# First modulation of a diffusion block: split products against plain fp32 products in four column groups

## Chip, core and metric

One NeuronCore of a Trainium2 chip runs the whole program. The metric is device time in microseconds (us) of one execution. The kernel before takes 2560.0 us, the median of 3 runs (2559.35 to 2563.09).

## What is computed

One layer of a diffusion backbone in fp32: 512 latent tokens (an 8 x 64 grid) and 256 context tokens of width 2048. A linear map of SiLU(c), or of SiLU(c_ctx) for the context, gives six vectors of 2048; the first two, shift and scale, modulate the input before the attention. That map, for these two vectors, is what the change touches.

```python
def ada_params(cond, w, b):
    return jnp.split(jax.nn.silu(cond) @ w + b, N_ADA, axis=-1)
def modulate(x, shift, scale):
    return x * (1 + scale) + shift
sh1, sc1, g1, sh2, sc2, g2 = ada_params(c, ada_w, ada_b)
csh1, csc1, ... = ada_params(c_ctx, ada_w, ada_b)
h, hc = modulate(x, sh1, sc1), modulate(ctx, csh1, csc1)
q, k, v = split(h @ w_qkv);  k_c, v_c = split(hc @ w_qkv[:, D_MODEL:])
x = layer_norm(alpha * x + g1 * (attention(q, k, v, k_c, v_c) @ w_o))
x = layer_norm(alpha * x + g2 * swiglu(modulate(x, sh2, sc2)))
```

## The kernel before

Everything is kept transposed, channels on partitions, in tiles of 128 channels; `kt` counts the 16 of them. Large products run as three matmuls on fp32r operands: each fp32 operand is split by `split` (lines 76 to 78) into a rounded part `hi` (a cast on ScalarE) and the rest `lo` (a subtraction on VectorE), and `mm3` adds hi*hi, hi*lo and lo*hi in PSUM. Weights arrive by `unit` (lines 103 to 106): a load of 128 x 1024 on SyncE's queue into one of six buffers of the pool `p0`, then the split into `wh_...` and `wl_...`, of which there are three each.

The first stage (lines 236 to 245) goes over `kt`. For each it needs shift and scale of 128 channels, for latent and context.

- `ada_start(kt)` (lines 182 to 193) computes them as rows. The stationary operand is `sil`, for each of the 16 tiles of the contraction four columns: SiLU(c) and SiLU(c_ctx), each as hi and lo part. The moving operand is 256 columns of the weights (128 shifts, 128 scales), once as hi and once as lo. That makes 4 units of weights and 32 matmuls into four rows of PSUM bank 7 (`adp`), copied by ScalarE to `row`.
- `ada_cols(kt)` (lines 195 to 205) turns the rows to columns by two transposes on TensorE, and two additions on VectorE join the hi and lo parts and the bias in `md`.
- `h_start(kt)` (lines 207 to 218) modulates 128 channels of x and of the context on VectorE and splits them (`a_h`, `hc`).
- `qkv_start(kt)` (lines 220 to 234) multiplies them with a 128 x 768 weight tile (`w0`; `wh_w`, `wl_w`) into seven banks `acc`: 12 matmuls of 512 columns, then 18 of 256.

The modulation of kt+1 stands ahead of the main products of kt, and `ada_cols(kt + 1)` between the 512-column and the 256-column ones:

```python
for kt in range(KT):
    h_start(kt)
    if kt + 1 < KT:
        ada_start(kt + 1)
    qkv_start(kt)
```

The framework's scheduler sets the final order of each engine's queue from this order and the buffers; it moves single instructions past each other, among them loads of the next stage's value weights (`wr_v`), which it puts among those of this stage.

Of the kernel before, what the change touches and what calls it, by code (L numbers as in the profile page):

```python
# [9 lines left out]
F32 = mybir.dt.float32  # L10
F32R = mybir.dt.float32r
AF = mybir.ActivationFunctionType
ALU = mybir.AluOpType
# [4 lines left out]
P = 128  # L18
D = 2048
KT = D // P  # L20
# [13 lines left out]
U = 1024  # L34
# [9 lines left out]
def build(tc, ins, out):  # L44
    nc = tc.nc
    with ExitStack() as top:
        base = top.enter_context(tc.tile_pool(name="base", bufs=1))
# [4 lines left out]
        def bank(i, name):  # L52
            return psp.tile([P, T], F32, tag=f"b{i}", name=name)
# [7 lines left out]
        def any_bank(name):  # L61
            turn["all"] += 1
            return bank((turn["all"] - 1) % 8, name)
# [12 lines left out]
        def split(hi, lo, src):  # L76
            nc.scalar.copy(hi, src)  # L77
            nc.vector.tensor_tensor(out=lo, in0=src, in1=hi.bitcast(F32), op=ALU.subtract)  # L78

        def mm(ps, a, b, start, stop):  # L80
            nc.tensor.matmul(ps, a, b, start=start, stop=stop, skip_group_check=True)  # L81
# [9 lines left out]
        def raw_tile(name, tag=None):  # L91
            if tag is None:
                tag = rtags[0][rtags[1] % len(rtags[0])]
                rtags[1] += 1
            return rp[0].tile([P, U], F32, tag=tag, name=f"wr_{name}", bufs=RAWBUFS.get(tag))

        def pieces(raw, name, n=U):
            hi = wp.tile([P, U], F32R, tag="whi", name=f"wh_{name}")
            lo = wp.tile([P, U], F32R, tag="wlo", name=f"wl_{name}")
            split(hi[:, :n], lo[:, :n], raw[:, :n])  # L100
            return hi, lo

        def unit(src, name, n=U):
            raw = raw_tile(name)
            nc.sync.dma_start(raw[:, :n], src)
            return pieces(raw, name, n)

        cv = base.tile([P, 2, KT], F32, name="cv")
        nc.sync.dma_start(cv, ins["cv"])
        nc.scalar.activation(cv, cv, AF.Silu)  # L110
        sil = base.tile([P, KT, 4], F32R, name="sil")
        for i in range(2):
            split(sil[:, :, 2 * i], sil[:, :, 2 * i + 1], cv[:, i])
        ada = base.tile([P, 64], F32, name="ada")
        ident = base.tile([P, P], F32, name="ident")
        make_identity(nc, ident)
        ones = base.tile([P, P], F32, name="ones")
        nc.gpsimd.memset(ones, 1.0 / D)
        eps_t = base.tile([P, 1], F32, name="eps_t")
# [3 lines left out]
        bin1 = base.tile([P, KT, 4], F32, name="bin1")  # L123
        bin2 = base.tile([P, 64], F32, name="bin2")

        def biases():
            nc.vector.tensor_copy(bin1, pv[:, 128:192].rearrange("p (k f) -> p k f", f=4))
            nc.vector.tensor_scalar_add(bin1[:, :, 2:4], bin1[:, :, 2:4], 1.0)
            nc.vector.tensor_copy(bin2, pv[:, 0:64])
            nc.vector.tensor_scalar_add(bin2[:, 32:48], bin2[:, 32:48], 1.0)  # L130
# [22 lines left out]
        with ExitStack() as ph1:  # L153
            pa = ph1.enter_context(tc.tile_pool(name="pa", bufs=1))
# [27 lines left out]
            def ada_start(kt):  # L182
                ps = bank(7, f"adp{kt}")
                for u in range(4):
                    hi, lo = unit(ins["ada_n"][kt, :, u * U:(u + 1) * U], f"an{kt}_{u}")
                    for jj in range(4):
                        j = u * 4 + jj
                        s_ = slice(jj * 256, jj * 256 + 256)
                        mm(ps[:4, :256], sil[:, j], hi[:, s_], j == 0, False)
                        mm(ps[:4, :256], sil[:, j], lo[:, s_], False, j == KT - 1)  # L190
                row = pa.tile([4, 256], F32, tag="row", name=f"row{kt}")
                nc.scalar.copy(row, ps[:4, :256])
                rows[kt] = (ps, row)

            def ada_cols(kt):
                ps, row = rows.pop(kt)
                pc = ps[:, 256:264].rearrange("p (f c h) -> p f c h", f=2, c=2)
                for i in range(2):
                    nc.tensor.transpose(ps[:, 256 + 4 * i:260 + 4 * i], row[:, i * P:(i + 1) * P], ident[:4, :4])
                md = pa.tile([P, 4], F32, tag="md", name=f"md{kt}", bufs=2)  # L200
                mdv = md.rearrange("p (f c) -> p f c", f=2)
                nc.vector.tensor_tensor(out=mdv, in0=pc[:, :, :, 0], in1=bin1[:, kt].rearrange("p (f c) -> p f c", f=2),
                                        op=ALU.add)
                nc.vector.tensor_tensor(out=mdv, in0=pc[:, :, :, 1], in1=mdv, op=ALU.add)
                mods[kt] = md

            def h_start(kt):
                md = mods.pop(kt)
                xr = stage(f"xr{kt}")
                nc.gpsimd.dma_start(xr, ins["xT"][kt])  # L210
                nc.vector.tensor_scalar(out=xr, in0=xr, scalar1=md[:, 2:3], scalar2=md[:, 0:1],
                                        op0=ALU.mult, op1=ALU.add)
                split(*new_act(kt, "h"), xr)
                cr = stage(f"cr{kt}")
                nc.gpsimd.dma_start(cr[:, :C], ins["ctxT"][kt])
                nc.vector.tensor_scalar(out=cr[:, :C], in0=cr[:, :C], scalar1=md[:, 3:4], scalar2=md[:, 1:2],
                                        op0=ALU.mult, op1=ALU.add)
                split(hc_hi[kt], hc_lo[kt], cr[:, :C])
# [16 lines left out]

            with tc.tile_pool(name="p0", bufs=6) as p0:
                rp[0] = p0
                ada_start(0)
                biases()
                ada_cols(0)  # L240
# [5 lines that stand above are left out]
# [173 lines left out]
            for hp in range(1, NH // 2):  # L419
# [6 lines left out]
                for i in range(2):  # L426
                    h = hp * 2 + i
# [42 lines left out]
        with ExitStack() as ph2:  # L470
# [96 lines left out]
            for n in range(KT - 1):  # L567
                if n < 3:
                    ps = ys[n]
                else:  # L570
                    ps = any_bank(f"y{n}")
# [5 lines left out]
            for cs in (HA, HB):  # L577
                ps = any_bank(f"y{KT - 1}_{cs.start}")[:, HA]
                for kt in range(KT):
                    hi, lo = hl[kt // 8]  # L580
                    s_ = slice(kt % 8 * P, kt % 8 * P + P)
# [327 lines left out]
            for cs in (HA, HB):  # L909
                for n in range(KT):  # L910
                    u = cu[n // 2][:, n % 2 * T:n % 2 * T + T]
# [68 lines left out]
```

## Time and profile before

| | |
|---|---|
| median of 3 runs | 2560.0 us (2559.35 to 2563.09) |
| profiled execution, its own time | 2558.94 us |
| its span in the trace | 2557.2 us |
| TensorE granted clock, mean | 0.987 |
| DMA | 395.66 MB, mean 155 GB/s |
| first stage (first product to last of `acc`) | 8.3 to 165.5 us |

The span is what the trace covers of the profiled execution. Engines: PE is TensorE's matmuls and PEld its weight loads, which overlap them; DVE is VectorE, ACT ScalarE, POOL GpSimd, SP SyncE. `L81` is line 81; since one helper records all matmuls, tile names tell them apart. A record's duration is its latency, and matmuls are pipelined: how fast they follow each other is read from their starts. `128*4` ahead of a shape is the stationary operand, partitions x columns.

### The profile page before, as it was taken

The numbers are of one execution on the slowest core, as the hardware profiler recorded it, in microseconds if no ns is written. First come the engines' busy times: TensorE is split into PE (matmuls) and PEld (weight loads), VectorE is DVE, ScalarE is ACT, GpSimd is POOL, SyncE is SP. The second block draws the span as 40 slices with busy tenths as digits, with TensorE's granted clock in tenths as the row PEclk, the third lists the DMA queues.
The fourth block names the chain that finished last, engine by engine and source line by source line (L and its number), as shares of the span: only waits on it lengthen the run. The fifth ranks groups of instructions, "written<-read, shape, count | busy, mean of one in ns | idle before, by whom it ended". The sixth has DMA issues, their size and how long they took to land.

```text
span 2557.2 us, 44451 instructions
## 1 busy us (share of the span) xinstructions
PE 2455.8 (96%) x18124; PEld 2305.1 (90%) x18124; DVE 1880.4 (74%) x2742; ACT 1074.9 (42%) x1640; POOL 220.6 (9%) x334
## 2 busy tenths in 40 slices
PE   8999999999999999999999999999999989999994
PEld 5788989898898987889999999999999989999984
DVE  7886665565565565459887887888878877878888
ACT  5662322222232244227544444444444534546444
POOL 1110000000010000001110110101101000000002
PEclk9999999999999999999999999999999999999997
DMA  9965454444444464214443334333444654755542
GB/s 332 308 211 168 148 165 133 156 160 151 154 157 156 144 234 145 92 64 141 148 141 117 134 127 138 131 122 130 138 138 160 201 173 126 214 146 159 133 121 75
DMA packets 137294, 395.66 MB, mean 155 GB/s; under 512 B 16416, under 2 KB 40368, under 8 KB 136960
## 3 DMA queue, kind: packets, MB, share of 16 engines
q1 hardware_dynamic: 116992, 342.42, 40.2%
q0 software_dynamic: 20096, 50.39, 7.2%
q8 instruction: 142, 2.33, 0.4%
q14 instruction: 64, 0.52, 0.1%
HBM read 351.85 MB, written 40.89 MB: 154 GB/s over the span
## 4 chain that ended last, share of the span: by engine, by line
PE 55%; issue 26%; DVE 9%; DMA 7%; ACT 2%; POOL 2%; SPq 0%; POOLq 0%; ACTq 0%; DVEq 0%
PE y L81 6%; DMA wr_ada<-ada_t 6%; PE qp L81 5%; PE kp L81 5%; PE vp L81 4%; PE acc L81 3%; PE cp L81 2%; DVE wr_ada L138 2%; PE o L81 1%; PE adp L81 1%; DVE wl_v L78 1%; PE f31b L81 1%; PE f28b L81 1%; PE f24b L81 1%; PE f21b L81 1%
## 5 line engine op out<-in xcount | busy, mean ns | idle before, releaser
L721 DVE TENSOR_TENSOR wr_f<-wr_f,wr_f 128x1024 f32<-128x1024 f32 x164 | 199.9, 1219 | 1.4
L81 PE MATMUL vp<-wh_v,a_h 128*128 128x256 f32 x896 | 167.9, 279 | 0.0
L81 PE MATMUL y<-a_o,wh_o 128*128 128x512 f32 (+1 forms) x544 | 163.0, 383 | 0.0
L138 DVE CUSTOM_DVE_ANT_0 wr_ada<-wr_ada,s_c,bin 128x1024 f32<-128x1024 f32 x64 | 83.5, 1304 | 86.8 <-DMA wr_ada<-ada_t 86.5
L81 PEld LDWEIGHTS vp<-wh_v,a_h 128*128 128x128 f32 x896 | 141.3, 188 | 0.6
L81 PE MATMUL kp<-a_h,wh_k 128*128 128x512 f32 x448 | 141.1, 396 | 0.0
L81 PE MATMUL qp<-a_h,wh_q 128*128 128x512 f32 x448 | 140.6, 395 | 0.0
L138 DVE CUSTOM_DVE_ANT_0 wr_ada<-wr_ada,s_c,adap 128x1024 f32<-128x1024 f32 x64 | 82.2, 1284 | 74.6 <-DMA wr_ada<-ada_t 74.5
L81 PE MATMUL vp<-wl_v,a_h 128*128 128x256 f32 x448 | 125.1, 279 | 0.0
L81 PEld LDWEIGHTS y<-a_o,wh_o 128*128 128x128 f32 x544 | 99.7, 188 | 21.7 <-ACT wh_o L77 0.7
L721 DVE TENSOR_TENSOR wr_g<-wr_g,wr_g 128x896 f32<-128x896 f32 (+1 forms) x96 | 107.6, 1131 | 6.1 <-DMA wr_g<-w_out 5.1
L77 ACT CAST th<-tr 128x256 fp32r<-128x256 f32 (+2 forms) x96 | 45.9, 478 | 151.4 <-PE tr L316 148.3
L81 PE MATMUL y<-a_o,wl_o 128*128 128x512 f32 (+1 forms) x272 | 104.0, 382 | 0.5 <-DVE wl_o L78 0.5
L81 PEld LDWEIGHTS cp<-hc,wh_k 128*128 128x128 f32 x448 | 84.1, 188 | 20.2
L81 PE MATMUL vp<-wh_v,hc 128*128 128x256 f32 x512 | 99.4, 283 | 0.0
L81 PEld LDWEIGHTS qp<-a_h,wh_q 128*128 128x128 f32 x448 | 82.1, 188 | 16.4
L634 POOL DMA_DIRECT2D setB<-h x66 | 35.6, 542 | 700.8 <-DVE h L773 689.0
L78 DVE TENSOR_TENSOR tl<-tr,th 128x256 fp32r<-128x256 f32 (+2 forms) x96 | 52.9, 552 | 54.3 <-ACT th L77 54.2
L81 PE MATMUL cp<-hc,wh_k 128*128 128x256 f32 x448 | 89.5, 281 | 0.0
L78 DVE TENSOR_TENSOR wl_an<-wr_an,wh_an 128x1024 fp32r<-128x1024 f32 x64 | 76.2, 1224 | 18.2 <-ACT wh_an L77 17.8
L81 PE MATMUL qp<-a_h,wl_q 128*128 128x512 f32 x224 | 88.6, 396 | 0.0
L299 ACT ACTIVATE p<-sc,sm 128x256 f32<-128x256 f32 x64 | 30.3, 474 | 138.4 <-DVE sm L297 138.3
(1666 smaller groups left out, 8461.0 us busy)
## 6 DMA issues: line engine op xcount, KB each, us to landing
wr_f<-w_in SPq DMA_DIRECT2D x164, 512.0 KB, 4.2
wr_ada<-ada_t SPq DMA_DIRECT2D x128, 512.0 KB, 4.0
wr_an<-ada_n SPq DMA_DIRECT2D x64, 512.0 KB, 6.2
wr_g<-w_out SPq DMA_DIRECT2D x64, 448.0 KB, 4.5
wr_v<-w_v SPq DMA_DIRECT2D x32, 512.0 KB, 4.7
wr_o<-w_o SPq DMA_DIRECT2D x32, 512.0 KB, 3.8
wr_g<-w_out SPq DMA_DIRECT2D x32, 512.0 KB, 4.3
wr_q<-w_qk SPq DMA_DIRECT2D x28, 512.0 KB, 4.5
```

The lines of the kernel that those rows point to most:

```text
L77: nc.scalar.copy(hi, src)
L78: nc.vector.tensor_tensor(out=lo, in0=src, in1=hi.bitcast(F32), op=ALU.subtract)
L81: nc.tensor.matmul(ps, a, b, start=start, stop=stop, skip_group_check=True)
L138: nc.vector.tensor_tensor_reduce(out=raw, in0=raw, in1=s_c[:, half * U:(half + 1) * U], scale=1.0, scalar=bin2[:, i:i + 1] if half == 0 el ...
L299: nc.scalar.activation(p[:, nl:nl + C], sc[:, :C], AF.Exp, bias=sm[:, 2:3], accum_out=sm[:, 3:4])
L634: nc.gpsimd.dma_start(setD[n][q], src)
L721: nc.vector.tensor_tensor(out=self.r[out][:, :n], in0=self.r[a][:, :n], in1=self.r[b][:, :n], op=op)
```

## The change

The weights of the first modulation are no longer split. The products are plain fp32. The 16 tiles of the contraction go in turn to four groups of 32 columns of the array: tile j = 4u + g is multiplied in group g and added up, over the units u, in the 32 rows of PSUM that begin at 32g. The stationary operand `sil` has 32 columns for each tile, the first two SiLU(c) and SiLU(c_ctx), the others zero, so that all 128 rows are written. `row` has 128 rows. In place of the two transposes stand two fp32 products with `sel`, a 128 x 2 matrix of zeros and ones that adds rows 0, 32, 64 and 96 into column 0 and rows 1, 33, 65 and 97 into column 1. One addition with the bias is left.

```diff
-        sil = base.tile([P, KT, 4], F32R, name="sil")
-        for i in range(2):
-            split(sil[:, :, 2 * i], sil[:, :, 2 * i + 1], cv[:, i])
...
+        sel = base.tile([P, 2], F32, name="sel")
+        nc.vector.tensor_tensor(out=sel, in0=ident[:, 0:2], in1=ident[:, 32:34], op=ALU.add)
+        for g in (64, 96):
+            nc.vector.tensor_tensor(out=sel, in0=sel, in1=ident[:, g:g + 2], op=ALU.add)
...
             def ada_start(kt):
                 ps = bank(7, f"adp{kt}")
                 for u in range(4):
-                    hi, lo = unit(ins["ada_n"][kt, :, u * U:(u + 1) * U], f"an{kt}_{u}")
-                    for jj in range(4):
-                        j = u * 4 + jj
-                        s_ = slice(jj * 256, jj * 256 + 256)
-                        mm(ps[:4, :256], sil[:, j], hi[:, s_], j == 0, False)
-                        mm(ps[:4, :256], sil[:, j], lo[:, s_], False, j == KT - 1)
-                row = pa.tile([4, 256], F32, tag="row", name=f"row{kt}")
-                nc.scalar.copy(row, ps[:4, :256])
+                    raw = raw_tile(f"an{kt}_{u}")
+                    nc.sync.dma_start(raw, ins["ada_n"][kt, :, u * U:(u + 1) * U])
+                    for g in range(4):
+                        mm(ps[32 * g:32 * g + 32, :256], sil[:, u * 4 + g], raw[:, g * 256:g * 256 + 256],
+                           u == 0, u == 3)
+                row = pa.tile([P, 256], F32, tag="row", name=f"row{kt}")
+                nc.scalar.copy(row, ps[:, :256])
                 rows[kt] = (ps, row)
...
                 for i in range(2):
-                    nc.tensor.transpose(ps[:, 256 + 4 * i:260 + 4 * i], row[:, i * P:(i + 1) * P], ident[:4, :4])
+                    mm(ps[:, 256 + 2 * i:258 + 2 * i], row[:, i * P:(i + 1) * P], sel, True, True)
                 md = pa.tile([P, 4], F32, tag="md", name=f"md{kt}", bufs=2)
-                mdv = md.rearrange("p (f c) -> p f c", f=2)
-                nc.vector.tensor_tensor(out=mdv, in0=pc[:, :, :, 0], in1=bin1[:, kt].rearrange("p (f c) -> p f c", f=2),
-                                        op=ALU.add)
-                nc.vector.tensor_tensor(out=mdv, in0=pc[:, :, :, 1], in1=mdv, op=ALU.add)
+                nc.vector.tensor_tensor(out=md, in0=ps[:, 256:260], in1=bin1[:, kt], op=ALU.add)
...
             with tc.tile_pool(name="p0", bufs=6) as p0:
                 rp[0] = p0
+                sil = p0.tile([P, KT, 32], F32, name="sil", bufs=1)
+                nc.gpsimd.memset(sil, 0.0)
+                for i in range(2):
+                    nc.vector.tensor_copy(sil[:, :, i], cv[:, i])
```

TensorE's queue before, where the main products of the first kt end and the modulation of the third begins (a row gives line, output and operands, the shape of the output, and how often it repeats):

```order
L81 MATMUL acc_126<-hc_89,wl_w_271 128x256
L81 MATMUL adp_319<-wh_an_0_322,sil 4x256
L81 MATMUL adp_319<-wl_an_0_323,sil 4x256
L81 MATMUL adp_319<-wh_an_0_322,sil 4x256
L81 MATMUL adp_319<-wl_an_0_323,sil 4x256
```

The same place with the change, up to the main products of the second kt and the selecting products among them:

```order
L81 MATMUL acc_125<-hc_88,wl_w_209 128x256
L81 MATMUL adp_256<-wr_an_0_257,sil 32x256 x4
L81 MATMUL adp_256<-wr_an_1_263,sil 32x256 x4
L81 MATMUL adp_256<-wr_an_2_269,sil 32x256 x4
L81 MATMUL adp_256<-wr_an_3_275,sil 32x256 x4
L81 MATMUL acc_119<-a_h,wh_w_285 128x512 x2
...
L81 MATMUL acc_122<-a_h,wl_w_286 128x512
L81 MATMUL adp_256<-sel,row_281 128x2 x2
L81 MATMUL acc_123<-wh_w_285,a_h 128x256
```

Eight products of two operands for each unit became four, one for each column group, which read the landed weights themselves.

VectorE's queue before, from the modulation of the second kt to that of the third (`an2` and `an3` are weight units, `w01` the main weights):

```order
L202 TENSOR_TENSOR md1_288<-adp1_209,bin1_86 128x4
L204 TENSOR_TENSOR md1_288<-adp1_209,md1_288 128x4
L211 TENSOR_SCALAR xr1_309<-xr1_309,md1_288 128x512
L216 TENSOR_SCALAR cr1_314<-cr1_314,md1_288 128x256
L78 TENSOR_TENSOR a0_h_201<-xr1_309,a0_h_201 128x512
L78 TENSOR_TENSOR hc0_89<-cr1_314,hc0_89 128x256
L78 TENSOR_TENSOR wl_an2_2_351<-wr_an2_2_348,wh_an2_2_350 128x1024
L78 TENSOR_TENSOR wl_an2_3_365<-wr_an2_3_362,wh_an2_3_364 128x1024
L78 TENSOR_TENSOR wl_w01_381<-wr_w01_378,wh_w01_380 128x768
L78 TENSOR_TENSOR wl_an3_0_433<-wr_an3_0_430,wh_an3_0_432 128x1024
L78 TENSOR_TENSOR wl_an3_1_447<-wr_an3_1_444,wh_an3_1_446 128x1024
```

And now, the whole round:

```order
L200 TENSOR_TENSOR md2_303<-adp2_256,bin1_85 128x4
L207 TENSOR_SCALAR xr2_323<-xr2_323,md2_303 128x512
L212 TENSOR_SCALAR cr2_328<-cr2_328,md2_303 128x256
L78 TENSOR_TENSOR a0_h_171<-xr2_323,a0_h_171 128x512
L78 TENSOR_TENSOR hc1_89<-cr2_328,hc1_89 128x256
L78 TENSOR_TENSOR wl_w02_363<-wr_w02_360,wh_w02_362 128x768
```

The four subtractions of 1024 columns and the second addition are gone from it. In SyncE's queue the three first loads of `wr_v`, which stood among the weight units of the modulation, now stand behind the last `wr_w` of the stage.

## Rows read from the trace of the kernel before

**Rows 1.** The page of the kernel before: busy us of each engine, share of the span, instructions.

```profile
PE 2455.8 (96%) x18124; PEld 2305.1 (90%) x18124; DVE 1880.4 (74%) x2742; ACT 1074.9 (42%) x1640; POOL 220.6 (9%) x334
```

**Rows 2.** Busy time per stretch; after each colon: length, engines, clock, DMA share, GB/s.

```profile
4.00:20.00 16.00, 9.81 (x52) 5.57 (x53) 10.62 (x18) 9.57 (x14) 0.00 (x0) 0.89 1.02 401
21.93:156.67 134.74, 129.50 (x902) 99.78 (x901) 110.86 (x156) 84.99 (x115) 15.51 (x30) 1.00 0.88 302
```

**Rows 3.** Instructions on tile adp: duration ns min/median/max, first and last start.

```profile
L81 PEld LDWEIGHTS adp<-wh_an,sil x256: 82/84/125, 8.3 to 155.3; 128*4 128x4 f32 x128
...
L192 ACT COPY row<-adp x16: 352/354/363, 14.6 to 156.7; 4x256 f32<-4x256 f32 x16
```

**Rows 4.** Timeline of TensorE, one kt; start us, duration us, idle before it.

```profile
42.90 0.63 PE L81 MATMUL acc<-a_h,wh_w 128*128 128x512 f32 x2
43.36 0.40 PE L81 MATMUL acc<-a_h,wl_w 128*128 128x512 f32 x1
43.69 0.28 PE L199 MATMUL adp<-ident,row 4*128 4x4 f32 x2
43.90 0.39 PE L81 MATMUL acc<-wh_w,a_h 128*128 128x256 f32 x1
...
46.01 0.28 PE L81 MATMUL acc<-hc,wl_w 128*128 128x256 f32 x1
46.13 0.28 PE L81 MATMUL adp<-wh_an,sil 128*4 128x256 f32 x1
...
47.96 0.28 PE L81 MATMUL adp<-wh_an,sil 128*4 128x256 f32 x1
48.62 0.28 PE L81 MATMUL adp<-wl_an,sil 128*4 128x256 f32 x1 [0.38 <-DVE wl_an L78]
...
49.43 0.28 PE L81 MATMUL adp<-wh_an,sil 128*4 128x256 f32 x1
49.54 0.40 PE L81 MATMUL acc<-a_h,wh_w 128*128 128x512 f32 x1
```

**Rows 5.** TensorE's waits, 22 to 160 us: us in total, times, longest.

```profile
PE adp L81 <- DVE wl_an L78: 5.2, 14, 0.4
```

**Rows 6.** Timeline of all engines, the start and the first kt.

```profile
5.78 1.04 ACT L77 CAST wh_an<-wr_an 128x1024 fp32r<-128x1024 f32 x1 [3.17 <-DMA wr_an<-ada_n]
...
8.33 0.37 PE L81 MATMUL adp<-wh_an,sil 128*4 128x256 f32 x1 [8.33 <-DVE sil L78]
...
11.07 1.05 ACT L77 CAST wh_an<-wr_an 128x1024 fp32r<-128x1024 f32 x1 [0.44 <-DMA wr_an<-ada_n]
...
14.59 0.35 ACT L192 COPY row<-adp 4x256 f32<-4x256 f32 x1
...
21.93 0.36 ACT L192 COPY row<-adp 4x256 f32<-4x256 f32 x1
```

**Rows 7.** Loads of tile wr_an and what is made from it.

```profile
L77 ACT CAST wh_an<-wr_an x64: 1039/1048/1053, 5.8 to 152.2; 128x1024 fp32r<-128x1024 f32 x64
L78 DVE TENSOR_TENSOR wl_an<-wr_an,wh_an x64: 1216/1226/1227, 6.9 to 153.5; 128x1024 fp32r<-128x1024 f32 x64
...
DMA to landing us min/median/max: 4.2/6.2/9.8
```

**Rows 8.** Matmuls whose operands are both fp32 (constant ones), 256 columns.

```profile
L81 PEld LDWEIGHTS mA<-lnA,ones x8: 187/190/190, 1138.8 to 1148.6; 128*128 128x128 f32 x8
L81 PE MATMUL mA<-lnA,ones x8: 377/379/379, 1138.9 to 1148.8; 128*128 128x256 f32 x8
1148.56 0.59 PE L81 MATMUL mA<-lnA,ones 128*128 128x256 f32 x2
...
1148.99 0.59 PE L81 MATMUL mA<-sqA,ones 128*128 128x256 f32 x2
```

**Rows 9.** Timeline, the chain from the transposes to the next operand.

```profile
44.08 0.16 DVE L202 TENSOR_TENSOR md<-adp,bin 128x4 f32<-128x4 f32 x1 [0.64 <-PE adp L199]
...
45.06 0.62 ACT L77 CAST a_h<-xr 128x512 fp32r<-128x512 f32 x1 [2.62 <-DVE xr L211]
```

More of the change, by code (lines that the diff above doesn't have):

```diff
@@ L196, in ada_cols @@
                 ps, row = rows.pop(kt)
-                pc = ps[:, 256:264].rearrange("p (f c h) -> p f c h", f=2, c=2)
                 for i in range(2):
-                    nc.tensor.transpose(ps[:, 256 + 4 * i:260 + 4 * i], row[:, i * P:(i + 1) * P], ident[:4, :4])
+                    mm(ps[:, 256 + 2 * i:258 + 2 * i], row[:, i * P:(i + 1) * P], sel, True, True)
                 md = pa.tile([P, 4], F32, tag="md", name=f"md{kt}", bufs=2)
-                mdv = md.rearrange("p (f c) -> p f c", f=2)
-                nc.vector.tensor_tensor(out=mdv, in0=pc[:, :, :, 0], in1=bin1[:, kt].rearrange("p (f c) -> p f c", f=2),
-                                        op=ALU.add)
-                nc.vector.tensor_tensor(out=mdv, in0=pc[:, :, :, 1], in1=mdv, op=ALU.add)
+                nc.vector.tensor_tensor(out=md, in0=ps[:, 256:260], in1=bin1[:, kt], op=ALU.add)
                 mods[kt] = md
```

## The prediction

> **What bounds the kernel now.** I read the engine line of the page first: TensorE is busy 96% of the span [rows 1], so a change pays by what it takes off TensorE's queue, or off a wait in that queue. The change touches only the first stage, so I went to the busy times by stretch next. Between the end of the second first-modulation product, 21.93 us, and the end of the sixteenth, 156.67 us, lie 14 equal rounds of 134.74/14 = 9.62 us [rows 2, 3, 6]. TensorE is busy 129.5 of the 134.7 us there at a granted clock of 1.00 (2.4 GHz), VectorE 110.9, ScalarE 85.0; DMA engines have a share of 0.88 at 302 GB/s [rows 2]. TensorE's order sets the round, VectorE is close behind it, and DMA is the next floor: a round loads 4 x 512 + 384 + 256 + 128 KB = 2.88 MB, which is 7.2 us at the 401 GB/s of the stretch from 4 to 20 us and 8.4 us at 302/0.88 = 343 GB/s [rows 2].
>
> In the timeline of one round the reader is to see three things. The 32 products of the modulation follow each other at 0.115 us (46.13 to 47.96 us are 16 steps, 48.62 to 49.43 seven) [rows 4]. There is one hole, 47.96 to 48.62, which is 0.54 us longer than a step and ends with VectorE's split of a weight unit; the table of waits counts 14 such waits, 5.2 us, which with the 0.165 us that each record outlasts its step is again 0.54 us a round [rows 4, 5]. And the two transposes cost 0.31 us: 43.36 to 43.90 less the 0.23 us of a 512-column product (two of them lie between 42.90 and 43.36) [rows 4].
>
> **The change, part by part.**
>
> *Products.* Removed: 32 x 0.115 = 3.68 us a round. Added: 16 plain fp32 products of 256 columns. No row shows such a product in a group of 32 columns. The nearest rows are the fp32 products with the constant ones: four products leave eight matmul records, so each makes two passes, and 1148.56 to 1148.99 is one product, 0.43 us, so 0.213 us a pass [rows 8]. One after the other the 16 would take 16 x 0.427 = 6.83 us; wholly side by side in fours 6.83/4 = 1.71 us. Those are the bounds. I take the middle one for a reason of order: the built order has the groups of a unit one after the other, and each product's second pass needs the same 32 columns as its first. If matmuls start in the order of the queue, as they do in every row here, the first pass of group g+1 can only start with the second pass of group g. That moves one product per pass: 16 x 0.213 + 0.21 for the last second pass = 3.62 us. The products alone thus gain 0.06 us a round; four times less array work turns into none.
>
> *The switch between products of 32 and of 128 columns.* It costs nothing in the rows: a four-column product follows a 128-column one 0.12 us later (46.01 to 46.13) and the way back is 0.11 us (49.43 to 49.54) [rows 4]. The Trainium skill (TensorEngine Tiling (Array Packing), Key Properties) says that changing the tiling mode drains TensorE. As built, the four-column products already stand in a 128 x 32 tile at column 0, so the trace does not agree with that page for this switch. By that rule the sum would come out at 2560, which is the third rival below.
>
> *The selecting product.* Two fp32 products of two columns replace two transposes: two passes each, so four loads of 128 stationary columns. A load of 128 columns lasts 188 ns against 84 for four columns [rows 3, 8], so about 0.104 us of a load is columns; 4 x 0.104 and one lead of about 0.1 is 0.5 us against 0.31: +0.2 us a round (bounds 0 and 0.4).
>
> *Splits.* 64 casts of 1.048 us leave ScalarE and 64 subtractions of 1.226 us leave VectorE [rows 7], about 145 us of engine time. On the path of the end lies only the hole: -0.54 us a round [rows 4, 5]. The rest was beside TensorE and is worth nothing, and so are the second addition per kt on VectorE, the wider row copy, and the two small set-ups (zeroing, selecting matrix): they lie ahead of the first landed weight at 5.78 us [rows 6]. A load buffer is now freed by TensorE's last read, not by VectorE up to three units ahead. The five loads of a round are then issued over about 3.5 us; with 6.2 us from issue to landing [rows 7] the last weight unit is there some 9 us after the start of one modulation, and it is read 9.2 + 2.6 us after it. Covered; were it not, each us late would be a us a round.
>
> *The chain to the next operand.* From the transposes at 43.69 to the addition at 44.08 and the end of the first operand's cast at 45.68 it is 2.0 us [rows 4, 9]; the context's cast, the weights' cast and the weights' subtraction follow, on fewer columns than the 1.05 and 1.23 us of the rows of 1024 columns [rows 7], so under 3.4 us together. Ahead of the next main products TensorE has 18 products, 43.90 to 46.13 [rows 4], and the modulation: 2.2 + 3.6 = 5.8 us. Covered; a modulation of 1.71 us would leave 3.9 and could uncover it. The loads of the next stage's value weights now follow the last weights of this stage in the queue. The buffers let them be issued over ten us before their use, so I cost that at nothing.
>
> *The start.* The first product waits until 8.33 us for the split, although its weights landed by 5.78; the fourth unit landed at 11.07, the first modulation ended at 14.59 and the second at 21.93 [rows 6]. Without splits the first ends about 11.07 + 5 x 0.213 = 12.1. The second needs four more units of 512 KB at 401 GB/s [rows 2], 1.3 us each, and its last products, 1.1 us: 17.4 us, or 19.4 if the inputs of two kt, 768 KB, come first. I take -2.5 us (bounds 0, if the lower clock of the start, 0.89 over 4 to 20 us [rows 2], costs it all, and -4.5).
>
> *Sum.* A round: -3.68 + 3.62 + 0.2 - 0.54 = -0.40 us, times 14 is -5.6; with the start -8.1 us. Against the profiled execution (span 2557.2, its own time 2558.94) that is 2550.8. The median of the three runs shown is 1.1 us higher, 2560.0, so the forecast is **2552 us**. The bounds above (start 0 to -4.5, selection 0 to 0.4) give 2547 to 2557.
>
> **The rivals.**
>
> *The groups run one after the other* (slower). Nothing in the trace shows two matmuls side by side in the array. Place: the modulation's products on TensorE. Price: 6.83 in place of 3.62 is +3.21 us a round, so +2.81 net; 14 x 2.81 = 39.3, and the start gives nothing back (about +1): **2600**, with 2596 to 2604. The point from which it decides: the round breaks even at 3.68 + 0.54 - 0.2 = 4.02 us for 16 products, 0.25 us each. For it: no row of a gain. Against it: the groups share neither columns nor output rows. Chance 0.26.
>
> *Four at a time* (faster). All four groups stream together and the modulation takes 1.71 us. The Trainium skill (TensorEngine Tiling (Array Packing), Theoretical Speedup) gives a factor of up to 4 for a dimension of 32 or less. No run here shows it. TensorE's round would be 9.62 - 0.40 - 1.91 = 7.3 us; DMA, at 7.2 to 8.4, becomes the bound, and with six buffers I take 8.1: 14 x 1.5 + 2.5 = 23.5, **2536** (2529 to 2545). Against it: two passes per product in queue order. The Trainium skill (TensorE: Matmul & The Clock Gate, Part 3) has matmuls strictly first in, first out, which speaks for the half. Chance 0.14.
>
> *Half overlap, but the switches drain.* A record of 0.28 us outlasts its step of 0.115 by 0.165, and a load of 0.084 to 0.188 follows [rows 3, 4, 8]: about 0.3 us, twice a round, 14 x 0.6 = 8.4 us, which eats the gain: **2560**. Against it stand the switches of 0.12 us in the trace. Chance 0.10.
>
> **How the numbers follow.** Half overlap has 0.50, the others 0.26, 0.14 and 0.10. The likeliest gives 2552, with 2547 to 2557 as its own range. From 2546 to 2604 the range holds it, the draining case and the slower rival, with 0.14 and a few tails left out below. A change under 0.2%, 5.1 us, can hardly be told from none: faster (below 2554.9) is 0.14 and 0.40 of the half, 0.54; the same is 0.10 of the half and 0.08 of the draining case, 0.18; slower is 0.26 and 0.02, 0.28.
>
> **What would show it.** In the profile after: modulation products that start 0.21 us apart (0.43 would show the slower rival, fours within 0.43 the faster one); no hole before them that ends with a split; 14 rounds of about 9.2 us between the second and the last row copy; the second row copy near 19 us; VectorE about 78 us and ScalarE about 67 us less busy; everything after the stage unchanged. I am wrong if the products' step is another, or if a new wait of TensorE on a landing of weights or on the row copy stands in the rounds.

## The result and the profile after

The changed kernel takes 2546.26 us, the median of four runs (2544.88 to 2548.09); the kernel before, on the same chip, 2559.68 (2556.47 to 2563.09). The ratio is 0.9945, with a 95% interval of 0.993 to 0.996: about 13 us, or half a per cent, faster. The forecast was 2552 with 2547 to 2557 as its own range. The result lies 0.7 us below that range, and it came about in another way than the forecast said.

| | before | after |
|---|---|---|
| profiled execution, its own time | 2558.94 | 2548.09 us |
| its span | 2557.2 | 2546.3 us |
| row copies, 1st, 2nd and 16th [rows 3, 6] | 14.6, 21.93, 156.7 | 12.1, 17.63, 141.4 us |
| round, mean over the last 13 additions to `md` | 9.55 | 8.76 us |
| last cast of the first stage's values starts (`v_2h`) | 166.1 | 153.4 us |

The engine line of the page, beside [rows 1], comes first: TensorE has 18 us less to do, VectorE 76, ScalarE 63.

```profile
PE 2437.6 (96%) x18156; PEld 2288.4 (90%) x18156; DVE 1804.6 (71%) x2665; ACT 1011.9 (40%) x1574; POOL 220.7 (9%) x335
```

The busy times by stretch answer to [rows 2]: the start, and the time from the second to the sixteenth row copy (columns as there).

```profile
4.00:20.00 16.00, 10.92 (x75) 4.85 (x76) 3.39 (x11) 2.40 (x5) 1.07 (x2) 1.00 1.01 397
17.63:141.40 123.77, 110.17 (x924) 83.06 (x924) 42.56 (x84) 30.31 (x58) 14.93 (x28) 0.99 0.92 330
```

The 14 rounds shrank from 134.74 to 123.77 us. TensorE was busy 96% of them before (129.50 of 134.74) and is busy 89% now (110.17 of 123.77): it lost 19 us of work, and 8 of them came back as waits. DMA moves 330 GB/s in place of 302.

TensorE's timeline of one kt, beside [rows 4], shows where the work went: the selecting products, the last main products, and the whole modulation as one row.

```profile
47.97 0.40 PE L81 MATMUL acc<-a_h,wl_w 128*128 128x512 f32 x1
48.20 0.50 PE L81 MATMUL adp<-sel,row 128*128 128x2 f32 x4
48.56 0.36 PE L81 MATMUL acc<-wh_w,a_h 128*128 128x256 f32 x1
...
50.64 0.28 PE L81 MATMUL acc<-hc,wl_w 128*128 128x256 f32 x1
50.85 1.93 PE L81 MATMUL adp<-wr_an,sil 128*32 128x256 f32 x32
52.91 0.50 PE L81 MATMUL acc<-a_h,wh_w 128*128 128x512 f32 x1
```

Sixteen products are 32 records, two passes each, and all of them fit in 1.93 us. The last record is 0.38 us long where the next would have followed after 0.22; less that tail of 0.16 it is 1.77 us, four products in 0.44 us, about what [rows 8] show for one (0.43). The four groups stream side by side. The busy times of the tile `adp` alone in two short stretches (columns as in [rows 2]; in brackets the number of records under way) show the order: four records begin within 0.05 us, and the next four only at 51.08 to 51.12.

```profile
50.84:50.89 0.05, 0.04 (x4) 0.04 (x6) 0.00 (x0) 0.00 (x0) 1.00 0.36 143
51.08:51.12 0.04, 0.04 (x8) 0.03 (x4) 0.00 (x0) 0.00 (x0) 1.00 1.02 410
```

The hole of [rows 4] is gone. From the last 512-column product to the first of 256 columns it is 48.56 - 47.97 = 0.59 us, less 0.23 for the product: the selection takes 0.36 us, where the transposes took 0.31.

The waits of TensorE and of those it waits for, from 22 to 155 us, beside [rows 5] (us in total, times, longest):

```profile
POOL xr L206 <- DVE a_h L78: 108.0, 14, 9.2
ACT wh_w L77 <- DMA wr_w<-w: 30.3, 14, 3.6
PE acc L81 <- ACT wh_w L77: 8.8, 8, 1.2
PE adp L81 <- DMA wr_an<-ada_n: 4.2, 8, 0.9
```

TensorE now waits for weights: 8.8 us for the main ones (their cast waits for the landing) and 4.2 us for those of the modulation. The first row is GpSimd's queue, which requests `xr`, the input x of the next kt: it stands still for 108 of the 133 us until VectorE has made the split of x of this kt (before the change for 115 of the 138 us from 22 to 160). VectorE's timeline, two rounds:

```profile
31.06 0.16 DVE L200 TENSOR_TENSOR md<-adp,bin 128x4 f32<-128x4 f32 x1 [5.09 <-PE adp L81]
...
38.48 0.16 DVE L200 TENSOR_TENSOR md<-adp,bin 128x4 f32<-128x4 f32 x1 [2.69 <-PE adp L81]
39.67 0.55 DVE L207 TENSOR_SCALAR xr<-xr,md 128x512 f32<-128x512 f32 x1 [1.03 <-DMA xr<-xT]
...
48.81 0.16 DVE L200 TENSOR_TENSOR md<-adp,bin 128x4 f32<-128x4 f32 x1 [2.58 <-PE adp L81]
```

One round is 7.42 us, the next 10.33; over the stage most short rounds of some 7.5 are followed by one of 9 to 11. In the second one `md` is there at 38.48, but x lands only at 39.67. GpSimd's timeline says when it was requested:

```profile
33.48 0.54 POOL L206 DMA_DIRECT2D xr<-xT  x1 [8.22 <-DVE a_h L78]
...
41.89 0.54 POOL L206 DMA_DIRECT2D xr<-xT  x1 [7.35 <-DVE a_h L78]
```

From one request to the next it is 8.41 us: 6.2 to the landing, then modulation, cast and split. Both x and the context's input go through two buffers of one tag (`stg`), in turn, so x of kt+1 gets its buffer only when x of kt is done with.

### The profile page after: what moved, and what is told of

Same layout as the page of the kernel before. It is cut to its first block, busy times and chain, and to the rows that moved or that the text cites. A ratio compares the mean times of both kernels' runs of the same rounds, so it can differ in the third digit from the quotient of the medians.

```text
span 2546.3 us, 44252 instructions
## 1 busy us (share of the span) xinstructions
PE 2437.6 (96%) x18156; PEld 2288.4 (90%) x18156; DVE 1804.6 (71%) x2665; ACT 1011.9 (40%) x1574; POOL 220.7 (9%) x335
## 4 chain that ended last, share of the span: by engine, by line
issue 37%; PE 17%; DVE 4%; POOL 3%; DMA 1%; ACT 1%; POOLq 0%; ACTq 0%; DVEq 0%; SPq 0%
PE y L81 6%; POOL setT L634 1%; POOL setB L634 1%; PE f4b L81 1%; PE f13b L81 1%; PE f9b L81 1%; PE f6b L81 1%; PE f14b L81 1%; PE f12b L81 1%; PE f11b L81 1%; PE f10b L81 1%; PE f8b L81 1%; PE f7b L81 1%; PE f5b L81 1%; PE f3b L81 1%
## 5 line engine op out<-in xcount | busy, mean ns | idle before, releaser
L81 PE MATMUL kp<-a_h,wl_k 128*128 128x512 f32 x224 | 88.4, 395 | 0.0
L299 ACT ACTIVATE p<-sc,sm 128x256 f32<-128x256 f32 x64 | 30.3, 473 | 138.3 <-DVE sm L297 138.1
```

Of the source, the lines that this page charges most:

```text
L299: nc.scalar.activation(p[:, nl:nl + C], sc[:, :C], AF.Exp, bias=sm[:, 2:3], accum_out=sm[:, 3:4])
```

## The experiments

Besides the ratio to the kernel before, the table has the mean round (last 13 additions to `md`) and the start of the last cast `v_2h` in the run's own trace, which is the end of the stage (before 9.55 and 166.1). The kernel before ran on the same chip each time; its medians there were 2565.6 to 2568.6 us, so times are compared on one chip. A ratio without an interval is one run.

| run | us | ratio to before | round | stage end |
|---|---|---|---|---|
| one column group | 2615.76 | 1.019 | 12.89 | 215.6 |
| two column groups | 2565.62 | 1.000 [0.9985, 1.0015] | 9.43 | 162.1 |
| four, group by group | 2594.74 | 1.011 | 10.54 | 188.2 |
| splits kept, unused | 2564.78 | 0.999 | 9.23 | 163.9 |
| the change again | 2557.30 | 0.9961 [0.9944, 0.9979] | 8.77 | 154.6 |
| own ring, main weights | 2555.98 | 0.9952 [0.9929, 0.9975] | 9.22 | 157.3 |
| ten weight buffers | 2560.24 | 0.997 | 8.91 | 154.4 |
| half the loads | 2556.64 | 0.995 | 9.01 | 153.9 |
| x apart | 2562.44 | 0.9984 [0.9971, 0.9996] | 9.06 | 157.2 |
| x apart, own ring | 2567.99 | 0.9999 [0.9987, 1.0011] | 9.05 | 158.1 |
| x apart, half the loads | 2543.94 | 0.991 | 7.71 | 138.3 |
| before, x apart | 2564.48 | 0.999 | 9.55 | 166.0 |
| x apart, ten buffers | 2551.48 | 0.9943 [0.9926, 0.9961] | 7.41 | 134.9 |
| x apart, 8 + 2 buffers | 2551.05 | 0.994 | 7.41 | 135.7 |
| the change, third time | 2559.19 | 0.9971 [0.996, 0.9981] | 8.93 | 155.5 |
| x apart, eight, mask ahead | 2552.39 | 0.9949 [0.9935, 0.9963] | 7.89 | 145.0 |

### Do the groups run side by side?

First theory: the 1.93 us are four groups at once. Three kernels change only which columns the products use, or their order. All products in columns 0 to 31 (and the selection over 32 rows):

```diff
-                        mm(ps[32 * g:32 * g + 32, :256], sil[:, u * 4 + g], raw[:, g * 256:g * 256 + 256],
-                           u == 0, u == 3)
+                        mm(ps[:32, :256], sil[:, u * 4 + g], raw[:, g * 256:g * 256 + 256],
+                           u == 0 and g == 0, u == 3 and g == 3)
```

> All 16 products of a kt go to columns 0 to 31; the rest is as in the changed kernel. Side by side (the groups share the array's time): 0.43 us a product, 6.8 us a modulation, a round of 2.2 + 2.8 + 0.5 + 6.8 = 12.4 us against 8.8, about 50 us slower than the changed kernel, 2596. Light product (a 32-column fp32 product takes 0.107 us wherever it stands): no change, 2546.

Two groups, g % 2:

```diff
+                        h = g % 2
+                        mm(ps[32 * h:32 * h + 32, :256], sil[:, u * 4 + g], raw[:, g * 256:g * 256 + 256],
+                           u == 0 and g < 2, u == 3 and g > 1)
```

> The products alternate between two groups. Side by side: 3.4 us a modulation, a round of about 9.1 us bound by TensorE, some 5 us slower than the changed kernel, 2551, near what was forecast for four groups. Light product: 2546.

Four groups, but all four products of a group behind each other in TensorE's queue:

```diff
+                for g in range(4):
+                    for u in range(4):
+                        mm(ps[32 * g:32 * g + 32, :256], sil[:, u * 4 + g], raws[u][:, g * 256:g * 256 + 256],
+                           u == 0, u == 3)
```

> Four groups, but the four products of one group stand next to each other in the queue, group after group. If TensorE takes matmuls strictly in queue order, only the products at the border of two groups overlap: about 6.2 us a modulation, 2588. If it can start a later product of another group ahead of one that waits for its own group: about 1.9 us, 2546 to 2550 (all four units must be there first).

The modulation of one kt in TensorE's timeline of these three, in this order; each row is the same 16 products:

```profile
67.37 7.09 PE L81 MATMUL adp<-wr_an,sil 128*32 128x256 f32 x32
```

```profile
62.91 3.65 PE L81 MATMUL adp<-wr_an,sil 128*32 128x256 f32 x32
```

```profile
63.54 4.59 PE L81 MATMUL adp<-wr_an,sil 128*32 128x256 f32 x32
```

7.09 us for one group (16 x 0.43 and a tail), 3.65 for two, 1.93 for four: the time goes with one over the number of groups. That settles the overlap. Two groups give just the 3.6 us that the prediction had forecast for four, a round of 9.43, and no difference in time that can be measured, although the stage ended 4 us earlier. (In that round the selecting product, over 64 rows, takes 0.27 us more than the change's; it is shown below with the switch between tiles.) The third row is more telling. If a product could start only when everything ahead of it in the queue has started, four products of one group behind each other would take their full time, and only where the queue passes from one group to the next could two overlap; that is over 6 us. If the order did not matter it would be 1.9. It took 4.59: TensorE does start products of another group past waiting ones, but only some way ahead. How far, the busy times of `adp` in this run say:

```profile
63.54:64.43 0.89, 0.89 (x4) 0.47 (x5) 0.00 (x0) 0.00 (x0) 1.00 1.05 426
64.44:64.45 0.01, 0.01 (x3) 0.01 (x2) 0.00 (x0) 0.00 (x0) 1.00 0.66 273
```

In the first 0.89 us only four records begin, passes of the first group, 0.22 us apart. At 64.44 three are under way: the fourth, the fifth, and the first of the second group, which begins right behind the fifth. The sixth to eighth pass of the first group are then still waiting. So the second group went ahead of three waiting passes and no more; the third and the fourth group follow at the same distance, and 3 x 0.89 + 1.93 is the 4.59 within 0.02. So the interleaved order of the change is part of its gain. (The run's rounds, 7.9 and 13.7 us in turn, also carry the wait for all four units before the first group can end.)

### What the lost splits are worth

The splits are made as before the change, and nothing reads them:

```diff
+                    pieces(raw, f"an{kt}_{u}")
```

> As the changed kernel, but each weight unit is still split by ScalarE and VectorE, and nothing reads the pieces. If the splits held only buffers and a wait of 0.54 us a round: rounds stay near 8.8 us, 2546 to 2549. If VectorE's queue is what the change relieved: rounds of 9.3 us and more, 2553 or above.

The round is 9.23 us, 0.3 to 0.5 more than in the three traces of the change (8.76, 8.77, 8.93), and the stage ends 8 to 11 us later. TensorE waits longer for ScalarE's cast of the main weights, which now stands behind casts of the modulation's:

```profile
PE acc L81 <- ACT wh_w L77: 17.6, 14, 2.1
```

14 waits, 17.6 us, against 8.8 (8 waits) in the change's first trace. This points to splits that do not stay beside TensorE's work once the modulation is short, at some 0.3 to 0.5 us a round. It is one run, and other variants below have rounds as long without the splits, so that price is an indication and not shown.

### Why a round is 8.8 us and not 7.4

By TensorE's own work a round should be 7.3 to 7.5 us. First suspects: the one ring of six weight buffers, and the bytes. Four kernels, the first of them the change itself again; the last loads two of the four units and reads each twice (1.84 MB a round, another output). The edits of the other three:

```diff
+        def main_tile(name):
+            return rp[0].tile([P, 768], F32, tag="wmain", name=f"wr_{name}", bufs=2)
...
-                wh, wl = unit(ins["w0"][kt], f"w0{kt}", 768)
+                raw = main_tile(f"w0{kt}")
+                nc.sync.dma_start(raw, ins["w0"][kt])
+                wh, wl = pieces(raw, f"w0{kt}", 768)
```

```diff
-            with tc.tile_pool(name="p0", bufs=6) as p0:
+            with tc.tile_pool(name="p0", bufs=10) as p0:
```

```diff
+                    if u % 2 == 0:
                         raw = raw_tile(f"an{kt}_{u}")
                         nc.sync.dma_start(raw, ins["ada_n"][kt, :, u * U:(u + 1) * U])
```

> The changed kernel once more, on this chip, as the measure for the next runs: 0.994 to 0.996 of the kernel before; modulations of about 1.9 us and rounds near 8.8 us, some of 7.5 and some of 9 to 11 us, the long ones with a wait for weights.

> The changed kernel with two buffers of their own for the main weights, so six are left for the modulation's (eight in all). Buffers bound the long rounds (a load is issued only when TensorE has read a buffer): rounds go to 7.5 to 7.9 us, 13 to 17 us faster than the changed kernel. The transfers themselves bound them (330 GB/s is what they reach): rounds stay near 8.8 us, no change.

> Ten common buffers in place of six; the first loads of the next stage then come behind a load that waits for the stage's end. Buffers: rounds of 7.5 to 7.9 us, but up to some us lost at the stage's end. Transfers: rounds of 8.8 us.

> Units 1 and 3 of the modulation's weights are not loaded; their products read units 0 and 2 once more (that part of the computation is left out). A round loads 1.88 MB in place of 2.88. Both theories: TensorE alone bounds the rounds, about 7.5 us. If rounds stay longer, something else than arriving weights holds them.

None of the three shortened the round (9.22, 8.91, 9.01). Not even half the loads did, with a DMA share of 0.58 in place of 0.93 (30 to 145 us). In that run the waits are for something else:

```profile
DVE xr L208 <- DMA xr<-xT: 32.2, 10, 4.4
PE acc L81 <- DVE a_h L78: 7.9, 10, 1.8
```

VectorE waits 32 us for x, and TensorE for its split. That turned the study to the two shared buffers. The second theory: the loop of x (request, landing, modulation, cast, split, next request) takes 8.4 to 9 us and is a floor of its own. Its edit gives x two buffers of its own; the context keeps `stg`:

```diff
-                xr = stage(f"xr{kt}")
+                xr = rp[0].tile([P, T], F32, tag="xr", name=f"xr{kt}", bufs=2)
```

It was tried alone, with the ring (five buffers and two for the main weights), with half the loads, and in the kernel before.

> The changed kernel, with two buffers of the input x of their own (before, x and the context's input take turns in two buffers, so that x of kt+1 is requested only after the last split of x of kt). Theory, the loop of x: a round of the changed kernel is 8.77 us because the request waits for the split, the load takes 6 to 7 us to land and modulation, cast and split another 2 us. With buffers of its own x is requested a round ahead, VectorE's wait for x goes, and a round falls to 8.0 to 8.4 us (the waits for weights stay): 5 to 10 us faster than the changed kernel, ratio to the kernel before about 0.992 to 0.994, where the changed kernel had 0.9961. Rival, the transfers: a round is 2.88 MB at the 330 GB/s that were seen; rounds stay at 8.7 to 9.2 us and the ratio at 0.996.

> The same with the main weights in two buffers of their own too, and five for the weights of the modulation. Theory of the loop: with both waits gone a round is TensorE's own 7.5 us, or DMA's 7.2 to 8.4: I expect 7.6 to 8.0, 10 to 15 us faster than the changed kernel, ratio 0.990 to 0.992. Rival, the transfers: no better than the changed kernel, 8.7 us or more.

> Own buffers for x, and two of the four weight units of each modulation not loaded (the other two are used twice, so its output is another): 1.88 MB a round. With half the loads but the shared buffers a round was 9.01 us. Theory of the loop: 7.4 to 7.6 us, TensorE without a wait, about 18 us less in the stage than the changed kernel. If x were not the cause it stays near 9.

> The kernel before the change, with own buffers for x. Theory of the loop: before the change it lay beside a TensorE round of 9.6 us and cost nothing: rounds stay at 9.55 us, no difference in time. If the loop had bound the round before too, it would fall.

In the kernel before it changed nothing (9.55 us), as the theory said. With half the loads the round fell to 7.71, most rounds 7.4 to 7.8. But alone, and with the ring, the expectation failed: 9.06 and 9.05. The waits of the run with x apart say where they went:

```profile
ACT wh_w L77 <- DMA wr_w<-w: 37.7, 14, 4.4
PE acc L81 <- ACT wh_w L77: 9.2, 9, 1.2
PE adp L81 <- DMA wr_an<-ada_n: 5.9, 10, 0.8
```

No wait for x is left in it, and those for weights are as long as in the change (15.1 us of TensorE's time, against 13.0 in the change's first trace). As whole kernels both were no faster than the change (0.9984 and 0.9999 of the kernel before, against 0.9945 to 0.9971). So there were two floors of about 9 us, one behind the other, and whoever lifts one finds the other. What was the second, the bytes or the late requests? Ten buffers together with x apart decide it, and eight for the modulation with two for the main weights.

> Own buffers for x, and ten instead of six buffers of weights; every load is done. Buffers theory: what is left of the waits with x freed (rounds of 9.06 us) is weights that are requested late, since SyncE's queue waits until TensorE has read a buffer; with ten buffers the requests run ahead and rounds fall to about 8.0 to 8.3 us, some 10 us off the stage. Transfer theory: 2.88 MB at the 320 to 335 GB/s of the rounds is 8.6 to 9.0 us whatever is requested when; after a few quick rounds, while the stock of buffers lasts, rounds go back to 8.6 us or more, and the mean from the third on is 8.4 to 8.9.

> The same with eight buffers for the modulation's weights and two for the main weights. Both theories as for ten common buffers; the separate ring would take away only the main weights' wait for the modulation's: within 0.2 us a round of that run.

VectorE's additions to `md` in the run with ten buffers, the third and fourth and the next to last:

```profile
32.10 0.16 DVE L200 TENSOR_TENSOR md<-adp,bin 128x4 f32<-128x4 f32 x1 [4.78 <-PE adp L81]
...
39.52 0.16 DVE L200 TENSOR_TENSOR md<-adp,bin 128x4 f32<-128x4 f32 x1 [3.99 <-PE adp L81]
...
121.14 0.16 DVE L200 TENSOR_TENSOR md<-adp,bin 128x4 f32<-128x4 f32 x1 [3.99 <-PE adp L81]
```

Twelve rounds of 7.42 us without an exception. The busy times of a stretch of it:

```profile
30.00:90.00 60.00, 60.00 (x533) 47.05 (x532) 24.14 (x48) 16.58 (x32) 8.53 (x16) 1.00 1.02 390
```

TensorE is busy 60.00 of 60 us, and DMA moves 390 GB/s. The buffers were the second floor, not the bytes: the expectation of the transfer theory (8.4 to 8.9) falls. SyncE requests a weight unit when TensorE has read the buffer; with six buffers and five tiles a round a request runs barely one round ahead, and with landings of 7.4 us (the change) and 7.9 us (x apart), both medians, that is too late as soon as a round is short. Ten buffers alone had not helped because x still held the round; x alone not because the weights did.

### Where the stage's gain goes

The rounds of 7.41 us ended the stage at 134.9 us, 18 to 21 us ahead of the change's traces (153.4, 154.6 and 155.5), yet the whole kernel gained a few us on it at most: 0.9943 of the kernel before, against 0.9945, 0.9961 and 0.9971 for the change on three chips. The next stage was not ready. Busy times around the seam, with ten buffers:

```profile
135.00:140.00 5.00, 0.98 (x9) 0.77 (x7) 0.94 (x3) 4.01 (x6) 0.00 (x0) 0.94 1.00 296
140.00:145.00 5.00, 1.28 (x4) 1.14 (x4) 0.43 (x2) 0.07 (x1) 3.01 (x4) 0.50 0.39 131
145.00:150.00 5.00, 3.75 (x15) 3.09 (x14) 4.36 (x10) 3.95 (x6) 0.00 (x0) 0.50 0.23 52
```

and the waits that fill it:

```profile
POOL mask L259 <- DVE hc L78: 14.1, 1, 14.1
PE sl L81 <- DVE sm L294: 7.7, 1, 7.7
DVE p L294 <- POOL bv L272: 7.1, 1, 7.1
```

TensorE stands for 7.7 us at the second score of the next stage, behind a softmax (`sm`, `p`) that waits for mask and bias (`bv`); the mask is requested when the first stage's buffers are given up. The granted clock is 0.50, the lower of the two levels (1.2 GHz), in the ten us from 140 to 150, so that what follows the wait runs at half speed too. By the first cast of the next values (`v_2h` from `vp`) 4.5 us of the 20 were left (215.2 against 219.7 in the change's second trace).

One more kernel has x apart, eight buffers, and the mask and bias tiles in a pool opened ahead of the stage, so that they are loaded during it; the change itself ran beside it.

```diff
+            pm = ph1.enter_context(tc.tile_pool(name="pm", bufs=1))
+            mask = pm.tile([P, 896], F32, name="mask")
+            with tc.tile_pool(name="p0", bufs=8) as p0:
...
-            nc.sync.dma_start(s_c, ins["c"].partition_broadcast(P))
+            nc.scalar.dma_start(s_c, ins["c"].partition_broadcast(P))
```

> The changed kernel as it is, beside the next on the same chip: ratio to the kernel before 0.994 to 0.996, rounds of 8.76 us.

> Own buffers for x, eight buffers of weights, and the mask and the bias tiles of the next stage in a pool of their own, so that they are loaded and summed during the first stage; the load of s_c goes to ScalarE's queue, out of the way of the value weights. With ten buffers the stage ended 18 us before the changed kernel's, but the next stage began with a wait of 7.7 us for the mask and the bias, and only some 4 us were left of it. Theory: that wait was the mask, which is requested when the first stage's buffers are given up; with it gone the rounds stay at 7.4 us and the run is 10 to 16 us faster than the changed kernel, ratio to before 0.988 to 0.991. Rival: the next stage then waits for its value weights instead, which are requested no earlier than with ten buffers (at the first stage's last kt), and no more than 4 us are gained, ratio about 0.994.

The wait for mask and bias shrank from 7.7 us to 0.6. But the rounds were 7.89 (from the eight common buffers, or from the loads of mask and bias that now fall into them; no run separates the two), and the gap at the seam stayed, smaller:

```profile
145.00:150.00 5.00, 2.68 (x9) 2.00 (x10) 3.13 (x9) 3.88 (x7) 0.00 (x0) 0.70 0.62 253
150.00:155.00 5.00, 5.00 (x28) 4.76 (x27) 4.71 (x9) 4.45 (x8) 0.00 (x0) 0.62 0.36 104
```

The timelines of ScalarE and TensorE in the same run show what is in it:

```profile
146.56 1.91 ACT L260 ACTIVATE s_c<-s_c 128x2048 f32<-128x2048 f32 x1 [1.12 <-DMA s_c<-c]
148.37 0.35 ACT L77 CAST k_h<-acc 128x256 fp32r<-128x256 f32 x1
...
149.15 2.96 ACT L77 CAST wh_v<-wr_v 128x1024 fp32r<-128x1024 f32 x3
```

```profile
146.09 0.35 PE L81 MATMUL sl<-k_h,q_h 128*128 128x256 f32 x1 [1.61 <-DVE k_l L78]
...
149.24 0.58 PE L81 MATMUL sc<-k_h,q_h 128*128 128x256 f32 x1 [0.60 <-DVE k_l L78]
```

Besides the 0.6 us for the softmax, TensorE's waits there end with VectorE's split of k. The second of these splits comes behind the cast of k at 148.37, and that stands behind the activation of `s_c`, which itself waited for its load. The value weights are cast only from 149.15 us; their request had gone out at 139.6, after the last kt. In the change's first trace two of these casts begin at 142.9 and 147.6, before its stage ends, and the value products start without a gap. So the first value product came at 151.3 here, hardly before the 152.4 of the change. The rival had named the value weights, and its number was nearer than the theory's: ratio 0.9949, 0.9935 to 0.9963, against 0.9971, 0.996 to 0.9981, for the change on the same chip. The intervals just overlap; the medians are 6.8 us apart. Its mechanism is not shown: at the seam TensorE waits for the split of a value weight only with a weight load and for 0.23 us, against 2.2 us for k, and what follows runs at a lower mean clock (0.70 and 0.62). This kernel seems some 0.2% faster than the change, at the edge of what these runs can tell; the version with ten buffers (0.9943) was not run on one chip with the change. Value weights in buffers of their own, requested during the last rounds, with `s_c` behind them, were not tried.

## Why the prediction was wrong, and where it was right

*Products: wrong.* The step that failed is "the first pass of group g+1 can only start with the second pass of group g". It gave 0.213 us a product and 3.62 us a modulation; measured is 0.11 us a product and 1.93 us with the tail. All four first passes run together, then all four second passes. The order in the queue is not the order of the starts across column groups: the run that stands group by group shows a group starting past three waiting passes of another. The Trainium skill (TensorE: Matmul & The Clock Gate, Part 3) states first in, first out; the prediction leaned on that, and here the measurement decides against it as a rule for products in different columns. The factor of up to 4 for a dimension of 32 or less (the Trainium skill, TensorEngine Tiling (Array Packing), Theoretical Speedup) is nearly what the runs gave: 7.09 us, 3.65, 1.93. The rival "four at a time" had the mechanism right and its price, 1.71 against 1.77 without the tail, at a chance of 0.14; its time, 2536, came out 10 us too low.

*The rounds: wrong, in the other direction.* With the true products the sum would have been -3.68 + 1.9 + 0.05 - 0.54 = -2.3 us a round; the runs without waits show 9.55 - 7.41 = -2.1. The change got -0.79. The 1.35 us between are the step "Covered": the prediction costed a later release of the weights' buffers, and the chain to the next operand, at nothing beside a modulation of 3.6 us, and said only that one of 1.71 could uncover the chain. It reckoned with 6.2 us from issue to landing, where the changed kernel's median is 7.4, and its own sign of being wrong, a new wait of TensorE on landings of weights, stands in the rounds (13.0 us). What came into the open was the loop behind the chain, the request for x, which no term contained, and then the buffers. The two errors have opposite signs (1.7 us a round too little for the products, 1.35 too much for what lies beside them), so that a forecast within 6 us of the result is luck. The rival's 8.1 us a round for DMA had neither: DMA ran at 390 GB/s when asked early enough, and the rounds stayed at 8.76 for want of early requests.

*Start: both times right, by two errors that cancel; the choice too cautious.* The first row copy was put at 12.1 and came at 12.11; the second at 17.4 to 19.4 and came at 17.63, so the start gave 4.3 us, not 2.5. But the prediction counted five passes of 0.213 us behind the last landing. TensorE's timeline has

```profile
10.96 1.08 PE L81 MATMUL adp<-wr_an,sil 128*32 128x256 f32 x8 [0.48 <-DMA wr_an<-ada_n]
...
13.86 3.64 PE L81 MATMUL adp<-wr_an,sil 128*32 128x256 f32 x32 [0.31 <-DVE md L200]
```

The second row is the 16 products that take 1.93 us at 50.85. So in the start four ran at a time, as later, but at half the pace. That is the pace of the lower clock (1.2 GHz), although the clock column says 1.00 for 4 to 20 us; there the rows decide.

*Splits: half right.* VectorE's and ScalarE's busy time fell by 76 and 63 us, near the 78 and 67 named. The prediction took only the hole from it. With the short modulation they may have cost 0.3 to 0.5 us a round more, by one run.

*Selection: +0.05 us, not +0.2,* within its bounds of 0 and 0.4. *The switch between tiles of 32 and of 128 columns* costs a little, about 0.1 us each way: entering, the first small product follows 0.21 us after the last full one (50.64 to 50.85) where the step is 0.12; leaving, TensorE's timeline of the run with ten buffers, weight loads included, has

```profile
50.30 0.61 PE L81 MATMUL adp<-wr_an,sil 128*32 128x256 f32 x8
50.84 1.00 PEld L81 LDWEIGHTS acc<-a_h,wh_w 128*128 128x128 f32 x5 [0.41 <-issue]
```

The last four products stream for 0.43 us, to 50.73; the full-width load starts only at 50.84, not under them as loads do elsewhere. The selecting product of the run with two groups is of the same type as the change's and has the same columns, but 64 rows, and takes 0.63 us (59.74 to 60.60 less 0.23) where the change's takes 0.36:

```profile
59.74 0.40 PE L81 MATMUL acc<-a_h,wl_w 128*128 128x512 f32 x1
60.06 0.60 PE L81 MATMUL adp<-sel,row 64*128 64x2 f32 x4
60.60 0.39 PE L81 MATMUL acc<-wh_w,a_h 128*128 128x256 f32 x1
```

The Trainium skill (TensorEngine Tiling (Array Packing), Key Properties) says that such a change of tile drains the array. The gaps in both places agree with it. About 0.1 us each way is small: a third of the 0.6 us a round that the draining rival assumed. Why the four-column products of [rows 4] had no such gap, no run here shows.

*The end.* To the last row copy the gain is 15.3 us (14 rounds x 0.78, and 4.3). At the end of the stage it is 12.7. In the last kt the addition to `md` comes 3.55 us after the row copy (2.0 before), and a split of value weights stands ahead of the modulation of x:

```profile
144.95 0.16 DVE L200 TENSOR_TENSOR md<-adp,bin 128x4 f32<-128x4 f32 x1 [1.50 <-PE adp L81]
145.03 1.23 DVE L78 TENSOR_TENSOR wl_v<-wr_v,wh_v 128x1024 fp32r<-128x1024 f32 x1
```

Of 12.7 us, 10.9 reach the end of the span. What happens between varies by some us from trace to trace, and no run here took it apart.

## What to carry to other kernels

Small stationary operands in separate column groups do run side by side, so a chain of narrow products is worth spreading over groups, in an order that goes round the groups. Before forecasting a round that gets shorter, write down every loop around a buffer (request, landing, use, release, next request) with its length: one that was hidden under the old round becomes the new one, and two of nearly the same length hide each other, so that freeing either alone shows nothing. And look at whether the stage behind can start earlier at all: here, of 20 us that a stage ended sooner, some 5 were left at the first values of the next.

## What the hardware did that was not expected

Two-pass fp32 products in four column groups take 0.43 to 0.44 us for four of them, as long as one alone. Within a group the products follow each other; across groups TensorE starts products past waiting ones, in the run group by group past three waiting passes and no more (4.59 us, between 1.93 and over 6).

Where TensorE had waited, the granted clock fell in some places, and part of the fall lay on the work that followed (0.50 in the ten us with and behind the end of the wait of 7.7 us, above). In its first trace the changed kernel has this once in its rounds, from 96 to 104 us, around waits of 0.6 and 1.2 us; its other waits there left the clock as it was. Before the change the mean clock of the rounds was 1.00 [rows 2]. The busy times around that fall:

```profile
96.00:100.00 4.00, 2.82 (x11) 2.12 (x8) 0.96 (x1) 1.10 (x2) 0.00 (x0) 0.72 0.93 308
100.00:104.00 4.00, 4.00 (x26) 3.58 (x26) 1.20 (x4) 0.82 (x2) 0.00 (x0) 0.85 0.97 378
```

So a wait can cost more than its own length.
